# Decoder layer on one core: the order of the modulation-weight loads in the DMA queue, and a ring of 24 slots for gate tiles

## The chip, the core and the metric

The kernel runs on one core of a Trainium2 chip. The core's engines work side by side, each on its own stream of instructions: TensorE (PE in the profile; its weight loads are PEld), VectorE (DVE), ScalarE (ACT), GpSimd (POOL) and SyncE (SP). In this kernel SP only issues DMAs (the loads of weights), and POOL issues nearly all other DMAs. The metric is the device time of one launch in microseconds (us); the three runs of the kernel before took 2658.97, 2663.2 and 2664.1 us, a median of 2663.2.

## The reference

One layer of a decoder, on 512 tokens of width 2048, everything in f32:

```python
mod = silu(c) @ w_ada + b_ada            # six vectors of 2048: shift, scale, gate, twice
h = rms_norm(x, g_attn) * (1 + sc_a) + sh_a
proj = h @ w_in                          # q/k/v and indexer of A, latents of B, gate_a, gate_b
o_a = dsa_attention(...)                 # branch A: attention over selected keys
o_b = causal_dense_attention(mq, mk, mv) # branch B: 8 heads of 128 (MLA)
merged = sigmoid(gate_a) * (o_a @ w_pa) + sigmoid(gate_b) * (o_b @ w_pb)
x = x + gt_a * (merged @ w_o)
h = rms_norm(x, g_ffn) * (1 + sc_f) + sh_f
x = x + gt_f * conv_ffn(h, w_up, w_conv, b_conv, w_down)
```

`w_ada` has 2048 rows and 12,288 columns, 100 MB; `w_pb` has 1024 rows and 2048 columns.

## The kernel before

**Products.** Each f32 operand is split into a high and a low part in a form that PE multiplies at full rate, and a product is three matmuls: high by high, high by low, low by high (`mm3`, L141 to 144). Activations lie transposed in tiles of 128x512, as pairs (hi, lo); `split` (L138 copies hi on ACT, L139 subtracts for lo on DVE) makes the pair. Weights come by `wtile` (L117): SP loads a raw tile of 128x1024 at high priority (L126), ACT copies its high part (L130), DVE subtracts for the low part (L131), and the raw buffer is free again. There are five raw buffers (`rawq`) and three hi/lo pairs.

**Memory.** Everything else lies in 81 slots of 128x512 f32, handed out by `get` (L69: the free slot that has rested longest) and given back by `put`. A slot taken again makes its new writer wait for the last reader of the old contents. PSUM has eight banks.

**Stages, in the order of time in the profile.** The input projection and branch A come first; at some 633 to 767 us the gate columns are projected; then come branch B's up projections and attention, head by head, with blocks of `w_pa` between the heads (`pa_block`, whose results pa go to DRAM); from about 955 to 1107 us the second branch, that is the four blocks of `w_pb` beside the last head; then `w_o`, the second norm, the up projection with convolution, and the down projection. The last two use a scheme of seven products for eight (`seven`), with its own load of weights (`load`).

**The ada stream.** `w_ada` is multiplied by one vector only, and on DVE instead of PE: `ada_stream` (L727) is a generator that loads two tiles of 128x512 at a time and adds each, times a column of silu(c), to an accumulator (L746 the first tile, L748 the others: 0.75 us each). In the second branch and in `w_o` the tiles go to slots (L736), first through a ring of six (`ada_ring`); earlier stages use raw buffers (L740). A `ticker` advances the stream by 1.25 pairs for each weight tile of `w_pb` and `w_o`.

**The last head.** `attend_p` (L677) computes, for four query blocks (512, 384, 256, 128 keys), the scores (PE, L1225 and L1226), adds the mask and takes the row's minimum on DVE (L689), exp and row sum on ACT (L690), reciprocal (L691) and scaling (L692) on DVE. `attend_pv` (L695) transposes on PE (L700), copies out of PSUM on DVE (L703) or ACT (L705), multiplies by the values (L708, "PV" below) and splits the result (L710, L711).

**The second branch.** `load_gates(cb)` (L1268) prepares four column blocks m: it loads pa (a), the gate of A (g) and the gate of B (b) from DRAM by POOL (L1274 to 1276, ordered behind the last store of pa for cb over 0), takes the sigmoids on ACT (L1279, L1280, ordered behind the last exp) and multiplies a by g on DVE (L1281), which frees g. After the product with `w_pb`, `ev_pb` (L1286) multiplies b by the bank (L1289), adds it to a (L1290), splits the sum into the merged pair and frees both tiles. All four calls of `load_gates` together load 48 tiles.

**What sets the order.** The program is written as one sequence. A scheduler reorders it when the kernel is built: it simulates the engines' time lines and picks for each engine the next instruction by priority (a raw tile's load, copy and subtraction have a raised one) among those that could start. The order on each engine is then fixed, and on the chip each engine runs its stream strictly in order. `tc.issue_after(x)` adds an edge for that scheduler: what is traced under it stands behind x.

Of the kernel before, what the change touches and what calls it, by code (L numbers as in the profile page):

```python
# [18 lines left out]
P = 128  # L19
# [12 lines left out]
def trunk_layer_kernel(  # L32
# [21 lines left out]
    V, A, G, PE, SP = nc.vector, nc.scalar, nc.gpsimd, nc.tensor, nc.sync  # L54
# [14 lines left out]
    def get(dt=F32):  # L69

        i = min(free, key=lambda n: rested[n])
        free.remove(i)
        if cur[i] is None or cur[i].dtype != dt:
            cur[i] = pool.tile([P, T], dt, name=f"slot{i}", tag=f"slot{i}")
        held[id(cur[i])] = i
        return cur[i]
# [4 lines left out]
    def put(*ts, lag=2):  # L81

        for t in ts:
            i = held.pop(id(t))
            rested[i] = clock[0] + lag
            free.append(i)
# [23 lines left out]

    weight_bufs(5, 3, 1104)

    def r32(ap):
        return ap.bitcast(F32)


    def wtile(src, k0, kg, c0, n, pri=PRI, more=None):  # L117
        i = cnt["wt"] % len(hi_b)
        cnt["wt"] += 1
        raw = rawq.popleft()  # L120
        w = kg * n
        if more:
            w += more[1]
        hi, lo = hi_b[i][:, :w], lo_b[i][:, :w]
        with tc.high_priority(offset=pri):
            SP.dma_start(raw[:, :kg * n].rearrange("p (k n) -> p k n", k=kg),  # L126
                         src[k0 * P:(k0 + kg) * P, c0:c0 + n].rearrange("(k p) n -> p k n", p=P))
            if more:
                SP.dma_start(raw[:, n:w], src[k0 * P:(k0 + 1) * P, more[0]:more[0] + more[1]])
            A.activation(hi, raw[:, :w], AF.Copy)  # L130
            V.tensor_tensor(lo, raw[:, :w], r32(hi), ALU.subtract)  # L131
        rawq.append(raw)
        if more:
            return hi, lo
        return (hi.rearrange("p (k n) -> p k n", k=kg), lo.rearrange("p (k n) -> p k n", k=kg))
# [141 lines left out]
    for ks in (range(0, 7), range(7, 14), range(14, KD)):  # L277
# [4 lines left out]
        for k in ks:  # L282
            t = get()
# [243 lines left out]
    b = bank[7]  # L527
# [199 lines left out]
    def ada_stream():  # L727
        for n, cb in enumerate(ada_blocks):
            assert len(pend) < 3
            acc = ada_acc[n % 3]  # L730
            for kp in range(8):
                if ada_in_slots[0]:
                    ts = [ada_ring.popleft(), ada_ring.popleft()] if ada_ring else [get(), get()]
                    for i in range(2):
                        k = kp * 2 + i
                        SP.dma_start(ts[i], w_ada[k * P:(k + 1) * P, cb * 512:(cb + 1) * 512])  # L736
                else:
                    raw = rawq.popleft()
                    t = raw[:, 0:1024].rearrange("p (k n) -> p k n", k=2)
                    SP.dma_start(t, w_ada[kp * 2 * P:(kp + 1) * 2 * P, cb * 512:(cb + 1) * 512]  # L740
                                 .rearrange("(k p) n -> p k n", p=P))
                    ts = [t[:, 0], t[:, 1]]
                for i in range(2):
                    k = kp * 2 + i
                    if k == 0:
                        V.tensor_scalar(acc, ts[i], c_act[:, 0:1], None, op0=ALU.mult)  # L746
                    else:
                        V.scalar_tensor_tensor(acc, ts[i], c_act[:, k:k + 1], acc,  # L748
                                               op0=ALU.mult, op1=ALU.add)
                if ada_ring_on[0]:  # L750
                    ada_ring.extend(ts)
                elif ada_in_slots[0]:
                    put(*ts)
                else:
                    rawq.append(raw)
                yield None
            pend.append((cb, acc))
            done[0] += 1
# [44 lines left out]
    def reload(d):  # L803
# [4 lines left out]
            G.dma_start(tl, dl)  # L808
            pairs.append((th, tl))
        return pairs  # L810

    last = {}


    gate_d = [dram.tile([P, T], F32, name=f"gate{k}") for k in range(2 * KD)]
# [132 lines left out]
    def seven(work, pairs_of_banks, hook=None, AHEAD=2):  # L948
        def pair_steps(n, p):
            bx, by = pairs_of_banks[n % len(pairs_of_banks)]  # L950
            X, Y, Z = bx[:, :HT], by[:, :HT], by[:, HT:]
            L, E = {}, {}
            W = p.K * P
            g1, g2 = p.scale or (None, None)
            r11, r21, r22, t1, t2, t3, t4 = p.rs

            def done(t):
                rawq.append(t)

            def load(blk):  # L960
                t = rawq.popleft()
                SP.dma_start(t[:, :W], p.load(blk))
                return t

            def hilo(t):
                i = cnt["wt"] % len(hi_b)
                cnt["wt"] += 1
                hi, lo = hi_b[i][:, :W], lo_b[i][:, :W]
                split(hi, lo, t[:, :W])
                return hi, lo  # L970

            def comb(o, a, b, op):
                V.tensor_tensor(o[:, :W], a[:, :W], b[:, :W], op)  # L973

            def copy(o, b, g):
                if g is not None:
                    A.activation(o, b, AF.Copy, scale=g)  # L977
                else:
                    A.activation(o, b, AF.Copy)

            def plus(o, b, g):
                if g is not None:
                    V.scalar_tensor_tensor(o, b, g, o, op0=ALU.mult, op1=ALU.add)
                else:
                    V.tensor_tensor(o, b, o, ALU.add)

            def p1():
                L[11] = load(0)
                L[21] = load(1)
                return hilo(L[11])  # L990

            def p7():

                s3 = rawq.pop()
                comb(s3, L[21], L[11], ALU.subtract)
                r = hilo(s3)
                done(s3)
                L[22] = load(3)
                return r

            def p6():
                comb(L[21], L[21], L[22], ALU.add)
                comb(L[11], L[21], L[11], ALU.subtract)
                r = hilo(L[11])
                L[12] = load(2)
                return r

            def p2():
                return hilo(L[12])

            def p5():
                r = hilo(L[21])
                comb(L[12], L[12], L[11], ALU.subtract)
                done(L[11])
                done(L[21])
                return r

            def p4():
                r = hilo(L[22])
                done(L[22])  # L1020
                return r

            def p3():
                r = hilo(L[12])
                done(L[12])
                return r

            def e1():
                E["u1"] = get()
                copy(E["u1"][:, :HT], X, g1)  # L1030

            def e7():
                E["u2"] = get()
                copy(E["u2"][:, HT:], Y, g2)

            def e6():
                copy(E["u2"][:, :HT], X, g2)

            def e2():
                plus(E["u1"][:, :HT], Z, g1)  # L1040

            def e5():
                plus(E["u2"][:, HT:], X, g2)

            def e4():
                plus(E["u2"][:, :HT], Y, g2)

            def e3():
                copy(E["u1"][:, HT:], X, g1)
                p.fin(E["u1"], E["u2"])  # L1050

            return ((p1, X, r11, e1, True), (p7, Y, t3, e7, True), (p6, X, t2, e6, False), (p2, Z, r21, e2, False),
                    (p5, X, t1, e5, False), (p4, Y, t4, e4, False), (p3, X, r22, e3, False))
# [211 lines left out]
    ob = reload(ob_d) + [tuple(att["o"][0:2]), tuple(att["o"][2:4])]  # L1265
    mg = []

    def load_gates(cb):  # L1268
        ts = []
        for m in range(4):  # L1270
            j = cb * 4 + m
            a, g, b = get(), get(), get()
            with tc.issue_after(last["store"].ins) if cb else nullcontext():
                G.dma_start(a, pa_d[j])  # L1274
                G.dma_start(g, gate_d[j])
                G.dma_start(b, gate_d[KD + j])

            with tc.issue_after(last["exp"].ins):
                A.activation(g, g, AF.Sigmoid)  # L1279
                A.activation(b, b, AF.Sigmoid)  # L1280
            V.tensor_tensor(a, a, g, ALU.mult)  # L1281
            put(g)
            ts.append((a, b))
        return ts

    def ev_pb(ts):  # L1286
        def ev(m, b):
            a, g = ts[m]
            V.tensor_tensor(g, g, b, ALU.mult)  # L1289
            V.tensor_tensor(a, a, g, ALU.add)  # L1290
            hi, lo = getr(), getr()
            split(hi, lo, a)
            put(a, g)
            mg.append((hi, lo))
        return ev

# [3 lines left out]
        lin_fm(w_pb, cb * 512, ob, 8, bk, ev_pb(load_gates(cb)), tick=ticker(TB))  # L1300
    for t in ob:
        put(*t)


    ss1 = pool.tile([P, 16], F32, name="ss1x")
# [334 lines left out]
```

## Time and profile before

| what | value |
|---|---|
| three runs | 2658.97, 2663.2, 2664.1 us |
| median | 2663.2 us |
| profiled execution | 2656.78 us |
| its span, first to last instruction | 2655.0 us |
| mean granted clock of PE | 0.990 |
| PE, DVE busy | 2588.7, 2174.6 us |
| moved by DMA | 464.31 MB |

The rows below are from that one profiled execution. A group's row holds the line, engine, operation, output and inputs (slot numbers left out), and the durations in ns (least, median, most). A wait's row says which engine's instruction at which line waited for which other one, for how many us in total, how often, and at most. A time line gives start and duration in us, and in brackets the idle time of the engine just before and what ended it. x3 stands for three like instructions in a row, shown as one stretch. PEclk is the clock granted to PE, 1.00 being full speed. A DMA's landing time runs from its issue to its arrival. Matmuls are pipelined, so their durations overlap; the distance between two starts is what one costs.

### The profile page before, as it was taken

The page shows a single profiled execution, that of the slowest core. Times are in us where ns is not written, and L with a number is a line of the kernel's source. Part 1 is how long each engine was busy: PE and PEld are TensorE (multiplying, and loading weights), DVE is VectorE, ACT ScalarE, POOL GpSimd, SP SyncE. Part 2 cuts the span into 40 slices and gives each one's busy share as a digit, 9 for nine tenths or more (in the row PEclk, how much of TensorE's full clock was granted, in tenths as well). Part 3 has the DMA queues.
Part 4 walks back from the last instruction along what each step waited for, and adds up shares of the span by engine and source line. Part 5 has one row for each costly group of instructions (what it writes and reads, how often), then busy time and mean ns, then how long its engine had stood idle before and what let it go on. Part 6 is the DMA issues. An engine that isn't in the chain of part 4 may idle for free.

```text
span 2655.0 us, 44904 instructions
## 1 busy us (share of the span) xinstructions
PE 2588.7 (98%) x17168; PEld 2344.2 (88%) x17168; DVE 2174.6 (82%) x3491; ACT 1243.0 (47%) x1953; POOL 365.8 (14%) x671
## 2 busy tenths in 40 slices
PE   6999999999999999999999999999999999999999
PEld 5777687778998877888789999999999999999999
DVE  7886975779878786983669899899899889878787
ACT  4333434334445544322544555555555556655454
POOL 1000011010023223200100000000001024413120
PEclk8999899999999999999999999999999999999999
DMA  9953136774676489873324434433434447867563
GB/s 342 340 165 101 35 101 192 224 215 150 203 240 190 153 274 354 299 238 95 135 74 143 135 124 129 137 123 129 136 123 150 142 146 217 219 155 202 143 208 114
DMA packets 215661, 464.31 MB, mean 175 GB/s; under 512 B 23786, under 2 KB 65156, under 8 KB 215444
## 3 DMA queue, kind: packets, MB, share of 16 engines
q1 hardware_dynamic: 170260, 344.93, 40.4%
q0 software_dynamic: 45152, 116.50, 15.0%
q8 instruction: 134, 2.20, 0.3%
q14 instruction: 83, 0.68, 0.1%
q10 hardware_dynamic: 32, 0.01, 0.0%
HBM read 397.11 MB, written 64.23 MB: 174 GB/s over the span
## 4 chain that ended last, share of the span: by engine, by line
PE 80%; issue 7%; DMA 6%; DVE 5%; ACT 1%; POOL 1%; SPq 0%; POOLq 0%; DVEq 0%; ACTq 0%
PE bank L1077 15%; PE bank L1079 15%; PE bank L1078 15%; PE bank L142 10%; PE bank L143 10%; PE bank L144 10%; DMA slot<-in_w_ada 3%; DVE whl L139 1%; DMA x<-slot 1%; PE bank L708 1%; PE bank L903 1%; DVE slot L572 0%; DMA raw<-in_w_ada 0%; PE bank L700 0%; DMA slot<-in_x 0%
## 5 line engine op out<-in xcount | busy, mean ns | idle before, releaser
L1077 PE MATMUL bank<-slot,whl 128*128 128x256 f32 x3920 | 1102.7, 282 | 21.0 <-ACT slot L977 6.1
L1078 PE MATMUL bank<-slot,whl 128*128 128x256 f32 x3920 | 1098.9, 281 | 0.2 <-DVE slot L139 0.2
L1079 PE MATMUL bank<-slot,whl 128*128 128x256 f32 x3920 | 1088.2, 281 | 6.0 <-DVE whl L139 6.0
L138 ACT ACTIVATE whl<-raw 128x1024 fp32r<-128x1024 f32 (+2 forms) x560 | 532.6, 953 | 618.2 <-PE bank L1078 400.7
L1077 PEld LDWEIGHTS bank<-slot,whl 128*128 128x128 f32 x3920 | 738.9, 189 | 28.2 <-ACT slot L977 8.6
L1078 PEld LDWEIGHTS bank<-slot,whl 128*128 128x128 f32 x3920 | 740.1, 189 | 0.6 <-DVE slot L139 0.5
L1079 PEld LDWEIGHTS bank<-slot,whl 128*128 128x128 f32 x3920 | 732.3, 188 | 7.2 <-DVE whl L139 7.2
L139 DVE TENSOR_TENSOR whl<-raw,whl 128x1024 fp32r<-128x1024 f32 (+2 forms) x560 | 606.0, 1087 | 121.2 <-ACT whl L138 116.9
L130 ACT ACTIVATE whl<-raw 128x1024 fp32r<-128x1024 f32 (+4 forms) x182 | 187.3, 1031 | 385.6 <-PE bank L144 193.8
L973 DVE TENSOR_TENSOR raw<-raw 128x1024 f32<-128x1024 f32 (+2 forms) x320 | 347.3, 1085 | 6.7 <-DMA raw<-in_w_ups 3.7
L131 DVE TENSOR_TENSOR whl<-raw,whl 128x1024 fp32r<-128x1024 f32 (+4 forms) x182 | 215.8, 1186 | 163.7 <-ACT whl L130 162.7
L143 PE MATMUL bank<-whl,slot 128*128 128x512 f32 (+2 forms) x768 | 297.3, 388 | 0.9 <-DVE whl L131 0.9
L142 PE MATMUL bank<-whl,slot 128*128 128x512 f32 (+2 forms) x768 | 293.1, 393 | 4.3 <-ACT slot L409 3.8
L144 PE MATMUL bank<-whl,slot 128*128 128x512 f32 (+2 forms) x768 | 292.9, 385 | 0.0
L142 PE MATMUL bank<-slot,whl 128*128 128x512 f32 (+1 forms) x656 | 264.1, 407 | 6.2 <-DVE slot L703 3.8
L143 PE MATMUL bank<-slot,whl 128*128 128x512 f32 (+1 forms) x656 | 266.0, 406 | 0.1
L144 PE MATMUL bank<-slot,whl 128*128 128x512 f32 (+1 forms) x656 | 258.0, 402 | 0.0
L748 DVE SCALAR_TENSOR_TENSOR slot<-slot,c_act,slot 128x512 f32<-128x512 f32 x203 | 150.9, 747 | 46.0 <-DMA slot<-in_w_ada 44.4
L142 PEld LDWEIGHTS bank<-whl,slot 128*128 128x128 f32 x768 | 146.0, 190 | 35.6 <-ACT slot L409 3.9
L143 PEld LDWEIGHTS bank<-whl,slot 128*128 128x128 f32 x768 | 146.3, 191 | 30.0 <-DVE whl L131 1.4
L144 PEld LDWEIGHTS bank<-whl,slot 128*128 128x128 f32 x768 | 144.7, 189 | 29.4 <-issue 0.5
L142 PEld LDWEIGHTS bank<-slot,whl 128*128 128x128 f32 (+1 forms) x656 | 123.7, 189 | 37.2 <-DVE slot L703 4.2
(288 smaller groups left out, 2705.5 us busy)
## 6 DMA issues: line engine op xcount, KB each, us to landing
slot<-in_w_ada SPq DMA_DIRECT2D x344, 256.0 KB, 5.4
raw<-in_w_ups SPq DMA_DIRECT2D x160, 512.0 KB, 5.1
raw<-in_w_in SPq DMA_DIRECT2D x50, 512.0 KB, 3.7
raw<-in_w_down SPq DMA_DIRECT2D x64, 384.0 KB, 3.8
raw<-in_w_down SPq DMA_DIRECT2D x64, 320.0 KB, 3.1
slot<-f POOLq DMA_DIRECT2D x154, 128.0 KB, 4.1
f<-slot POOLq DMA_DIRECT2D x66, 256.0 KB, 5.1
raw<-in_w_gs SPq DMA_DIRECT2D x32, 512.0 KB, 3.9
```

The costliest lines, as they stand in the source:

```text
L130: A.activation(hi, raw[:, :w], AF.Copy)
L131: V.tensor_tensor(lo, raw[:, :w], r32(hi), ALU.subtract)
L138: A.activation(dst_hi, src, AF.Copy)
L139: V.tensor_tensor(dst_lo, src, r32(dst_hi), ALU.subtract)
L142: PE.matmul(o, lh, rh, start=first, stop=False)
L143: PE.matmul(o, lh, rl, start=False, stop=False)
L144: PE.matmul(o, ll, rh, start=False, stop=last)
L748: V.scalar_tensor_tensor(acc, ts[i], c_act[:, k:k + 1], acc, op0=ALU.mult, op1=ALU.add)
L973: V.tensor_tensor(o[:, :W], a[:, :W], b[:, :W], op)
L1077: PE.matmul(o, wh[:, ks], rh, start=first and k == 0, stop=False, skip_group_check=True)
L1078: PE.matmul(o, wh[:, ks], rl, start=False, stop=False, skip_group_check=True)
L1079: PE.matmul(o, wl[:, ks], rh, start=False, stop=last, skip_group_check=True)
```

## The change

Two edits. First, the SP instruction that loads the newest weight tile is kept in `last["w"]`, in `wtile` (L126) and in the load of `seven`, and each ada load into a slot (L736) is traced behind it, with an ordering edge on SP. Ada loads into raw buffers (L740) have no edge. Second, the a, g and b tiles of `load_gates` no longer come from `get()` one by one: 24 slots are taken at once into `gate_ring`, tiles are taken from its left end, and g goes back to its right end after L1281, a and b after the block's evacuation; behind the four blocks the ring is given back as a whole. All other tiles of that stage have 24 slots fewer to rotate through while the ring is held.

```diff
+    last = {}
+
...
-            SP.dma_start(raw[:, :kg * n].rearrange("p (k n) -> p k n", k=kg),
+            last["w"] = SP.dma_start(raw[:, :kg * n].rearrange("p (k n) -> p k n", k=kg),
                          src[k0 * P:(k0 + kg) * P, c0:c0 + n].rearrange("(k p) n -> p k n", p=P))
...
                     for i in range(2):
                         k = kp * 2 + i
-                        SP.dma_start(ts[i], w_ada[k * P:(k + 1) * P, cb * 512:(cb + 1) * 512])
+
+                        with tc.issue_after(last["w"].ins):
+                            SP.dma_start(ts[i], w_ada[k * P:(k + 1) * P, cb * 512:(cb + 1) * 512])
...
-    last = {}
-
...
             def load(blk):
                 t = rawq.popleft()
-                SP.dma_start(t[:, :W], p.load(blk))
+                last["w"] = SP.dma_start(t[:, :W], p.load(blk))
                 return t
...
+    gate_ring = deque(get() for _ in range(24))
+
     def load_gates(cb):
         ts = []
         for m in range(4):
             j = cb * 4 + m
-            a, g, b = get(), get(), get()
+            a, g, b = (gate_ring.popleft() for _ in range(3))
...
             V.tensor_tensor(a, a, g, ALU.mult)
-            put(g)
+            gate_ring.append(g)
             ts.append((a, b))
         return ts
...
             split(hi, lo, a)
-            put(a, g)
+            gate_ring.extend((a, g))
             mg.append((hi, lo))
         return ev
...
     for t in ob:
         put(*t)
+    put(*gate_ring)
```

## The prediction

> **What bounds the kernel now.** I read the page's line of engines first, then busy time by stage, then what TensorE (PE) waited for in the stretch that the edit touches, and at last the instructions around the longest of those waits.
>
> ```profile
> span 2655.0 us, 44904 instructions
> ...
> PE 2588.7 (98%) x17168; PEld 2344.2 (88%) x17168; DVE 2174.6 (82%) x3491; ACT 1243.0 (47%) x1953; POOL 365.8 (14%) x671
> ```
>
> PE is the bound, with 98% of the span; all the engines together can give back only the remaining 66 us. The next view holds stages: from its start in us to its end, length, busy time and instructions of each engine, granted clock, DMA share, GB/s.
>
> ```profile
> 700.00:767.00 67.00, 66.41 (x560) 66.12 (x559) 58.08 (x67) 27.62 (x36) 6.72 (x13) 1.00 0.60 192
> 860.00:955.00 95.00, 94.97 (x466) 76.79 (x465) 73.80 (x223) 47.60 (x107) 22.12 (x33) 1.00 0.54 168
> 955.00:1000.00 45.00, 44.89 (x195) 33.57 (x194) 38.45 (x75) 16.01 (x31) 8.99 (x17) 1.00 0.94 306
> 1000.00:1030.00 30.00, 28.73 (x128) 21.62 (x126) 20.39 (x44) 11.82 (x24) 15.71 (x30) 1.00 1.06 394
> 1030.00:1060.00 30.00, 26.51 (x103) 20.70 (x104) 19.42 (x29) 14.70 (x24) 6.98 (x13) 0.89 0.93 343
> 1060.00:1107.00 47.00, 47.00 (x203) 37.78 (x203) 45.76 (x70) 21.77 (x32) 14.65 (x25) 1.00 0.81 258
> 1150.00:1200.00 50.00, 50.00 (x216) 40.35 (x215) 44.73 (x65) 15.10 (x25) 0.00 (x0) 1.00 0.68 225
> 2200.00:2250.00 50.00, 45.92 (x376) 44.87 (x377) 47.72 (x76) 32.94 (x58) 17.79 (x29) 1.00 0.76 207
> ```
>
> The second branch runs from about 955 to 1107 us. PE stands still there for 1.27 us in 1000:1030 and 3.49 us in 1030:1060, and in the latter its clock falls to 0.89; just there the DMAs move 394 GB/s. Elsewhere in the table PE is full, but for 4.08 us in 2200:2250. In 1060:1107 it starts 203 matmuls in 47.00 us: 0.2315 us each, my unit for what PE can cover. PE's two waits in that stretch:
>
> ```profile
> PE bank L142 <- DVE slot L703: 3.8, 1, 3.8
> PE bank L700 <- DVE slot L692: 0.9, 1, 0.9
> ```
>
> Both belong to the last attention head. PE itself, then VectorE (DVE), then ScalarE (ACT), each row with start, duration, and in brackets the idle time before it:
>
> ```profile
> 1016.61 0.38 PE L700 MATMUL bank<-ident,slot 128*128 128x128 f32 x2
> ...
> 1028.49 0.66 PE L700 MATMUL bank<-ident,slot 128*128 128x128 f32 x4 [0.88 <-DVE slot L692]
> ...
> 1033.42 0.79 PE L142 MATMUL bank<-slot,whl 128*128 128x512 f32 x1 [3.82 <-DVE slot L703]
> 1034.01 0.63 PE L143 MATMUL bank<-slot,whl 128*128 128x512 f32 x1
> ...
> 1037.85 0.40 PE L142 MATMUL bank<-slot,whl 128*128 128x512 f32 x1
> ```
> ```profile
> 1000.09 1.22 DVE L131 TENSOR_TENSOR whl<-raw,whl 128x1024 fp32r<-128x1024 f32 x1
> ...
> 1005.58 0.74 DVE L689 CUSTOM_DVE_ANT_0 slot<-bank,slot,nsc_b 128x512 f32<-128x512 f32 x1
> ...
> 1025.63 0.75 DVE L748 SCALAR_TENSOR_TENSOR slot<-slot,c_act,slot 128x512 f32<-128x512 f32 x1 [1.52 <-DMA slot<-in_w_ada]
> 1026.30 0.15 DVE L691 RECIPROCAL ri<-su 128x1 f32<-128x1 f32 x1
> 1027.48 0.75 DVE L748 SCALAR_TENSOR_TENSOR slot<-slot,c_act,slot 128x512 f32<-128x512 f32 x1 [1.03 <-DMA slot<-in_w_ada]
> 1028.15 0.28 DVE L692 TENSOR_SCALAR slot<-slot,ri 128x128 f32<-128x128 f32 x1
> ...
> 1031.21 0.75 DVE L748 SCALAR_TENSOR_TENSOR slot<-slot,c_act,slot 128x512 f32<-128x512 f32 x1 [0.51 <-DMA slot<-in_w_ada]
> ...
> 1033.08 0.28 DVE L703 COPY slot<-bank 128x128 f32<-128x128 f32 x1
> ```
> ```profile
> 1024.45 0.19 ACT L690 ACTIVATION_READ_ACCUMULATOR slot<-slot,mn 128x1 f32 x1
> 1024.65 1.28 ACT L1280 ACT_TABLE_LOAD   x1
> ...
> 1027.53 0.62 ACT L1280 ACTIVATE slot<-slot 128x512 f32<-128x512 f32 x1
> 1028.05 0.62 ACT L1279 ACTIVATE slot<-slot 128x512 f32<-128x512 f32 x1
> ```
>
> The last exp ends at 1024.64. The reciprocal and the scaling (0.15 + 0.28 us) could follow, but two ada accumulations (L748) stand ahead of them on DVE and idle 1.52 and 1.03 us for their DMAs; so the scaling starts at 1028.15, and the copy L703 at 1033.08. PE waits for both. Why those tiles are late, from the DMA views: landing time of ada loads issued in 995:1030, of gate loads over the whole run, of gate loads in 1055:1080 when the burst is over, and the queues of 1000:1040 (packets, MB, share; q0 is POOL's, q1 SP's).
>
> ```profile
> DMA to landing us min/median/max: 7.2/12.2/17.8
> ```
> ```profile
> DMA to landing us min/median/max: 3.0/7.9/8.8
> ```
> ```profile
> DMA to landing us min/median/max: 3.0/3.0/3.1
> ```
> ```profile
> DMA packets 6340, 15.69 MB, mean 392 GB/s; under 512 B 901, under 2 KB 901, under 8 KB 6338
> ...
> q0 software_dynamic: 3323, 10.09, 66.5%
> q1 hardware_dynamic: 3015, 5.57, 38.8%
> ```
>
> An ada tile takes 12.2 us while POOL pours out pa and gate tiles; POOL gets 10.09 MB through, SP 5.57 MB.
>
> **The change, part by part.** No instruction is added or removed on any engine, and no byte; what moves is order. In the built order the streams differ on PE, DVE, ACT, POOL and SP mainly in what runs at about 633 to 1290 us, and a little at the start of the down projection.
>
> *The last head's stall.* In the changed build the last reciprocal and scaling follow the last exp with no L748 between, so the 0.88 us go. Before the copy L703 stand now two L1281 and two L748, and PE has 13 matmuls (3.0 us) between the head's last transposes and the one that needs L703's bank, against 2 before. ACT starts a sigmoid every 0.52 us after its 1.28 us table load; the second L1281 needs the seventh, which ends some 5 us after the exp. The four transposes stand 27 matmuls (6.25 us) behind the last scores, some 3 us after the exp; 3.0 us of cover more is 6 us, so L703 comes about in time. I take the 3.82 us as gone; if its two L748 wait as those above did, up to 3 us come back. With that idle stretch goes the slow clock: from 1033.42 to 1037.85 PE starts ten matmuls in 4.43 us, where ten of 0.2315 take 2.3: 2.1 us. Together −0.88 −3.82 −2.1 = **−6.8 us**.
>
> [...]
>
> *Ada loads behind the last weight load (SP).* Before, ada loads stood ahead of weight loads in SP's queue; now each waits in that queue behind the newest weight load, and that load waits for its raw buffer, freed by L131 on DVE. Queued behind it are ada tiles alone, and DVE's L748 waits for those. Between the first and the last w_pb load stand 34 ada loads, before 42; six loads that were fetched ahead of w_pb come after its first tile. These 14 tiles, 14 x 0.75 = 10.5 us of DVE work, go to the w_o stage. There, in 1150:1200, DVE is idle 5.27 of 50 us; w_o has 768 matmuls, 178 us, so about 18.8 us are free: cost nothing; without that cover at most 10.5 us.
>
> The new hazard is the last head's start: three L748 whose tiles are queued behind the eighth w_pb load now stand ahead of its first L689. That load's buffer comes free when L131 of the third w_pb tile ends, at 1001.31 by the DVE row above, and SP issues the load at once. SP's issues and the sizes:
>
> ```profile
> 1001.33 0.38 SPq L126 DMA_DIRECT2D raw<-in_w_pb  x1
> ```
> ```profile
> L736 SPq DMA_DIRECT2D slot<-in_w_ada x17: 327/328/328, 995.5 to 1028.3; - x17
> ```
> ```profile
> slot<-in_w_ada SPq DMA_DIRECT2D x16, 256.0 KB, 13.9
> ...
> raw<-in_w_pb SPq DMA_DIRECT2D x4, 512.0 KB, 13.7
> ```
>
> Add 0.4 us for its issue and 0.7 for two ada issues, the landing L, 3 x 0.75 for L748, and about 3.5 us for three L689 (0.74 the widest), exp, reciprocal and scaling: 1008.2 + L. The transposes that need it started at 1016.61 without a wait, and stand about six matmuls (1.4 us) earlier in the new order, so L over 7.0 us costs what it is over. The third tile needs 0.52 + 3 x 0.26 MB through SP: by SP's average of 5.57 MB in 40 us that is 9.4 us, by the whole 392 GB/s with a 3 us floor some 6. The ends are then 0 (L of 7.0 or less) and +10.8 (L of 17.8); I take 7.7, since at first about 16 gate and pa tiles are queued and not 36: **+0.7 us**.
>
> *The ring (POOL).* The 48 a, g and b tiles used any free slot; 24 slots hold the first 24, the rest wait for L1281, L1290 or the last head's PV to release theirs. Two chains follow the last PV. (a) The low half of the seventh w_pb tile (L131) stands on DVE now behind four L1289, two L1290 and one L1281. PE has 44 matmuls (10.2 us) and 0.4 us of small ones before it needs it. The chain starts when the second bank is full, 20 matmuls (4.6 us) after PV; seven operations at 0.68 and L131's 1.22 follow:
>
> ```profile
> L1290 DVE TENSOR_TENSOR slot<-slot,slot x14: 681/683/685, 1059.3 to 1106.3; 128x512 f32<-128x512 f32 x14
> ```
>
> That is 4.6 + 4.8 + 1.2 = 10.6, and about 0.5 for the flush and semaphores: **+0.5 us**. (b) One gate tile of the first quarter reuses a slot that this PV reads. Its landing L, then sigmoid 0.62, L1289, two L1290, L1281 and L131 make about 5.7 + L against 10.6: break-even 4.9. The row nearest is the 3.0 us of gates loaded after the burst: nothing; at the burst's 8.8 it is +3.9.
>
> *Everything else.* In the stages at 700:767, 860:955 and 1150:1200 PE is full to within 0.6 us in the rows above, whatever stands in what order on the other engines; I take 0, bounded by ±2 us. The down projection's start: 0, bounded by the 4.08 us idle of its 50 us either way.
>
> Sum: −6.8 + 0.7 + 0.5 = −5.6 us, a span of 2649.4. The profiled execution took 2656.78 us, 1.78 beyond its span, and becomes 2651.2; it lies 6.4 below the median of the three runs, so on the median **2657.6 us**.
>
> **The rivals.** *The stall stays, under another L748.* [...] Then 3 of the 3.82 us come back, with the slow clock (about 1.5 of the 2.1), and 1.2 are paid: −6.8 + 4.5 + 1.2 = −1.1, 2662.1 us. Against it: 16 instead of 36 POOL tiles in the first burst. [...]
>
> *Slower: the last head starts late.* The L748 behind the eighth w_pb load hold up L689. It decides from an ada landing of 7.0 us on, and outweighs the gain from about 13. At the 17.8 us of the worst tile before, +10.8, and the late gate tile +3.9 beside it: −6.8 + 10.8 + 3.9 + 0.5 = +8.4, 2671.6 us. For it: a median of 12.2 us in just this stretch before. Against it: those medians came with twice the POOL tiles queued.
>
> *It doesn't do what it says.* The build's order shows 34 ada loads for 42, so the edges bind; no chance of its own.
>
> **How the numbers follow.** Forecast 0.45, stall stays 0.29, late head 0.26. About 0.2% (5.3 us) is what a measurement of this kernel can tell from no change: faster is below 2657.9, slower above 2668.5. The forecast's own range, 2653 to 2661, has about 0.33 below the bound and 0.12 in it; the stall staying gives 0.04, 0.22 and 0.03; the late head, with its price from nothing to 10.8, 0.02 in the middle and 0.24 above. Rounded: faster 0.38, same 0.35, slower 0.27. The range goes from 2651 (both new terms at nothing, 2 us from other stages, and a reading 3 us low) to 2671.
>
> **What would show it.** In the changed kernel's profile: the waits L142 on L703 and L700 on L692 are gone, and the clock in 1030:1060 is 1.00; ada landing times in 995:1030 have a median below 10 us; the second branch ends near 1101 instead of 1107. Wrong: a wait of L700 on L692 or of scores on L689 early in the last head, with DVE idle before L748 (late head); a wait on L131 well over 0.5 us after the last PV (late gate); a wait on L703 of 2 us or more (the stall stays); a PE wait in w_o on what L748 holds up.

## The result, and the profile after

The changed kernel is slower: 2676.45 us (median of 6 runs, 2674.52 to 2680.13) against 2660.32 us for the kernel before in the same measurement, a ratio of 1.0064 with a 95% interval of [1.0052, 1.0076]. The forecast was 2657.6 us, a small gain, with a range from 2651 to 2671.

Lines in the changed kernel stand 3 lower up to L735, then 5 lower up to L811, then 3 again, and 6 or 7 from the gate code (L1268) on: L131 is L134, L689 to L692 are L692 to L695, L703 is L706, PV's L708 is L711, L736 is L741, L748 is L753, L793 is L798, L973 is L976, L985 is L988. First the page's two lines of the changed kernel, then its busy time by stage (columns as before).

```profile
span 2673.5 us, 44893 instructions
...
PE 2599.5 (97%) x17168; PEld 2355.0 (88%) x17168; DVE 2175.3 (81%) x3491; ACT 1243.5 (47%) x1953; POOL 367.9 (14%) x671
```
```profile
630.00:790.00 160.00, 152.89 (x1232) 149.59 (x1233) 130.81 (x151) 65.32 (x86) 13.93 (x26) 0.98 0.60 195
955.00:1000.00 45.00, 43.72 (x191) 32.71 (x189) 27.22 (x58) 14.60 (x29) 7.04 (x13) 1.00 0.83 257
1000.00:1030.00 30.00, 25.21 (x101) 18.32 (x101) 17.21 (x39) 7.35 (x16) 10.18 (x19) 0.93 0.90 297
1030.00:1060.00 30.00, 28.51 (x118) 22.45 (x119) 20.20 (x42) 18.00 (x33) 9.57 (x18) 0.90 0.74 253
```

PE runs the same 17,168 instructions, is busy 10.8 us longer (most of it is the slow clock: 0.987 granted on average against 0.990 makes about 8 us) and idle 7.7 us longer; together the 18.5 us of the span. The same stretch of the kernel before for the first row of stages:

```profile
630.00:790.00 160.00, 156.63 (x1285) 154.60 (x1285) 134.73 (x155) 67.02 (x88) 18.88 (x36) 0.98 0.66 210
```

The reader is to see two things. PE gets through 53 matmuls less in 630:790, the gate projection, a stage for which I had forecast no change. And in 1000:1030 the DMAs are less busy than before (297 GB/s, 394 before), yet PE stands still for 4.79 us where it had been 1.27. Crowded DMAs are not the trouble any more. The ada loads issued in 995:1030 land faster, too, with a median below 10 us, as the forecast had it (7.2/12.2/17.8 us before):

```profile
DMA to landing us min/median/max: 4.9/7.2/9.4
```

What counts, as the next views show, is when they are issued.

To place the loss, I compare the start of the PE instruction with the same number in both traces; both run 17,168. The table gives that difference against the kernel before in us; the column heads name the experiments below. Each column is one execution, and the first row shows scatter alone: up to 631 us the changed kernel runs the order of before.

| PE instruction (start before) | changed | e1 | e2 | e3 | e5 | e9 |
|---|---|---|---|---|---|---|
| 2500 (560) | +1.8 | -0.5 | +0.3 | +0.6 | -0.1 | +0.7 |
| 4500 (871) | +8.9 | +8.8 | +1.4 | +2.9 | -2.3 | +0.3 |
| 5000 (979) | +8.4 | +9.1 | +1.4 | +2.8 | -2.6 | +0.2 |
| 5500 (1102) | +13.2 | +9.3 | -4.4 | +5.7 | +2.9 | -7.2 |
| 13500 (2199) | +14.1 | +7.5 | -4.7 | +6.3 | +4.6 | -8.5 |
| 14000 (2265) | +18.3 | +8.7 | -2.3 | +7.8 | +5.1 | -5.9 |
| 17000 (2631) | +18.6 | +9.5 | -1.8 | +8.7 | +6.0 | -4.6 |

The changed kernel loses in three places: 7.1 us between 560 and 871 us, 4.8 between 979 and 1102 (the second branch), and 4.2 between 2199 and 2265 (the start of the down projection). `w_o`, between 1107 and 1300 us, is flat.

**The last head.** PE's waits in 955:1115 of the changed kernel:

```profile
PE bank L145 <- DVE slot L798: 4.5, 1, 4.5
PE bank L711 <- DVE slot L706: 2.7, 1, 2.7
PE bank L146 <- DVE slot L714: 0.3, 1, 0.3
```

The two waits of before (on L703's bank, and of the transposes on the scaling) are gone, as forecast; other waits have come. DVE, SP and PE around the longest, each in its own view:

```profile
1014.85 1.22 DVE L134 TENSOR_TENSOR whl<-raw,whl 128x1024 fp32r<-128x1024 f32 x1
...
1017.30 0.28 DVE L706 COPY slot<-bank 128x128 f32<-128x128 f32 x1
1024.59 0.75 DVE L753 SCALAR_TENSOR_TENSOR slot<-slot,c_act,slot 128x512 f32<-128x512 f32 x1 [7.00 <-DMA slot<-in_w_ada]
1026.52 0.75 DVE L753 SCALAR_TENSOR_TENSOR slot<-slot,c_act,slot 128x512 f32<-128x512 f32 x1 [1.18 <-DMA slot<-in_w_ada]
1028.60 0.75 DVE L753 SCALAR_TENSOR_TENSOR slot<-slot,c_act,slot 128x512 f32<-128x512 f32 x1 [1.33 <-DMA slot<-in_w_ada]
1029.27 0.74 DVE L692 CUSTOM_DVE_ANT_0 slot<-bank,slot,nsc_b 128x512 f32<-128x512 f32 x1
...
1030.47 0.69 DVE L798 TENSOR_TENSOR slot<-bank,ident 128x512 f32<-128x512 f32 x1
```
```profile
1016.10 0.38 SPq L129 DMA_DIRECT2D raw<-in_w_pb  x1
1016.52 2.82 SPq L741 DMA_DIRECT2D slot<-in_w_ada  x4
```
```profile
1031.22 0.80 PE L145 MATMUL bank<-slot,whl 128*128 128x512 f32 x1 [4.54 <-DVE slot L798]
1031.81 0.63 PE L146 MATMUL bank<-slot,whl 128*128 128x512 f32 x1
```

This is a closed loop, and it reads off the three views. DVE ends the low part of a weight tile at 1016.07; that frees the raw buffer. At 1016.10 SP, which had stood 7.0 us, issues the next weight load, and at 1016.52, behind it, the ada loads that the edge holds back. The third of the tiles that DVE needs is there only at 1028.60. DVE reaches its L748 (L753 here) at 1017.6, stands there 7.00 + 1.18 + 1.33 us, and the last head's minimum and a column flush that PE's next bank needs stand behind. Tying the load to the weight load tied it to DVE's own progress.

**The gate projection.** A like chain, near 760 us in DVE, SP and PE:

```profile
757.80 1.22 DVE L976 TENSOR_TENSOR raw<-raw 128x1024 f32<-128x1024 f32 x1
...
761.08 0.75 DVE L753 SCALAR_TENSOR_TENSOR slot<-slot,c_act,slot 128x512 f32<-128x512 f32 x1 [0.92 <-DMA slot<-in_w_ada]
764.76 0.75 DVE L753 SCALAR_TENSOR_TENSOR slot<-slot,c_act,slot 128x512 f32<-128x512 f32 x1 [2.92 <-DMA slot<-in_w_ada]
765.43 0.42 DVE L988 TENSOR_TENSOR slot<-bank,slot 128x256 f32<-128x256 f32 x1
```
```profile
759.09 0.33 SPq L965 DMA_DIRECT2D raw<-in_w_gs  x1
759.51 0.86 SPq L741 DMA_DIRECT2D slot<-in_w_ada  x2
```
```profile
765.99 0.36 PE L1080 MATMUL bank<-slot,whl 128*128 128x256 f32 x1 [2.25 <-DVE slot L988]
```

L973 (L976) ends at 759.02, the weight load follows at 759.09, the ada loads at 759.51, DVE waits for the second until 764.76, and the evacuation L985 (L988), for which PE waits, stands behind it. Here, though, the buffer is the smaller part. SP's waits in 755:764 show that SP stood 5.1 us for the store out of the slot that the ada load at 758.38 overwrites, and only 0.3 us for the buffer:

```profile
SPq L741 <- DMA gate<-slot: 5.1, 1, 5.1
SPq L965 <- DVE raw L976: 0.3, 1, 0.3
```

Such stores hold SP up in the kernel before as well (25.2 us in 630:790, 22.8 after), so this one place doesn't show what the edge costs in this stage; e1, e3 and e5 below do. What DVE idled for ada tiles in slots, in 630:790 and in 955:1107, before and then after, sums it up (us, times, longest):

```profile
DVE slot L748 <- DMA slot<-in_w_ada: 12.2, 10, 4.7
...
DVE slot L748 <- DMA slot<-in_w_ada: 13.6, 10, 3.4
```
```profile
DVE slot L753 <- DMA slot<-in_w_ada: 19.7, 15, 2.9
...
DVE slot L753 <- DMA slot<-in_w_ada: 27.1, 10, 7.0
```

### The profile page after: what moved, and what is told of

The parts are those of the page before. It is cut to its first block, busy times and chain, and to the rows that moved or that the text cites. A ratio compares the mean times of both kernels' runs of the same rounds, so it can differ in the third digit from the quotient of the medians.

```text
span 2673.5 us, 44893 instructions
## 1 busy us (share of the span) xinstructions
PE 2599.5 (97%) x17168; PEld 2355.0 (88%) x17168; DVE 2175.3 (81%) x3491; ACT 1243.5 (47%) x1953; POOL 367.9 (14%) x671
## 4 chain that ended last, share of the span: by engine, by line
PE 64%; DVE 5%; DMA 5%; issue 2%; ACT 1%; POOL 0%; SPq 0%; DVEq 0%; ACTq 0%; POOLq 0%
PE bank L1080 15%; PE bank L1081 15%; PE bank L1082 15%; PE bank L145 6%; PE bank L146 6%; PE bank L147 6%; DMA slot<-in_w_ada 3%; DVE whl L142 2%; DVE raw L976 1%; DMA x<-slot 1%; ACT whl L141 1%; PE bank L1229 1%; PE bank L1228 1%; DVE slot L753 0%; PE bank L711 0%
## 5 line engine op out<-in xcount | busy, mean ns | idle before, releaser
L976 DVE TENSOR_TENSOR raw<-raw 128x1024 f32<-128x1024 f32 (+2 forms) x320 | 348.0, 1088 | 7.2 <-DMA raw<-in_w_ups 4.2
L133 ACT ACTIVATE whl<-raw 128x1024 fp32r<-128x1024 f32 (+4 forms) x182 | 187.1, 1030 | 350.8 <-PE bank L147 188.1
L134 DVE TENSOR_TENSOR whl<-raw,whl 128x1024 fp32r<-128x1024 f32 (+4 forms) x182 | 216.7, 1191 | 139.3 <-ACT whl L133 138.2
L753 DVE SCALAR_TENSOR_TENSOR slot<-slot,c_act,slot 128x512 f32<-128x512 f32 x203 | 151.7, 750 | 82.4 <-DMA slot<-in_w_ada 80.8
```

Source lines behind the costliest of these rows:

```text
L753: V.scalar_tensor_tensor(acc, ts[i], c_act[:, k:k + 1], acc, op0=ALU.mult, op1=ALU.add)
```

## The experiments

**Which part, and where.** Four kernels. In e1 the edge holds only until the second branch and there is no ring; e2 is the ring alone; e3 is the changed kernel with the edge only from the second branch on; e4 has both places of the edge and no ring.

```diff
 e1, e3 (condition on the edge; e1 has "not", e1 and e4 also take the ring out)
-                        with tc.issue_after(last["w"].ins):
+                        with tc.issue_after(last["w"].ins) if not ada_ring_on[0] else nullcontext():
```

> Only the ada loads of the gate projection (633 to 767 us) stand behind the last weight load; the second branch, w_o and the gate tiles are as before. Theory (three separate losses, one of them there): about 2660.3 + 6.5 = 2667 us, all of it gained between the matmuls that stood at 617 and 775 us before, and the difference constant after that. Rival (the ring and what follows from it make the whole loss, and that stage's loss in the one profile was chance): 2660, within 0.2%.

Measured: 2665.37 us, ratio 1.0031 [1.0019, 1.0044]; the table has the whole loss before 871 us. DVE's idle time for ada tiles in 630:790 and in 955:1107:

```profile
DVE slot L753 <- DMA slot<-in_w_ada: 21.3, 13, 5.4
...
DVE slot L753 <- DMA slot<-in_w_ada: 13.3, 9, 3.2
```

The first is close to that of the changed kernel (19.7), the second to that of before (13.6). The edge alone makes that stage's loss, without the ring.

How much one execution says can be read off the kernels that run this stage in one and the same order. With the edge, the start of instruction 4500 against that of 2500 moves by +7.1 us (changed), +9.3 (e1), +8.7 (e4), +12.8 (e6) and +12.1 (e10); without it, against the kernel before, by +1.1 (e2) and +2.3 (e3). The loss is clear of the scatter; its size is known to some 3 us only.

> Only the ring of 24 slots; no ada load is ordered behind a weight load. Theory (the ordering edges make the losses before 1107 us): the gate projection is as before, the last head keeps about the 6.8 us of before, and at the start of the down projection the order differs, for 0 to +4 us: 2658 to 2665. Rival (the ring's late tiles and the 24 slots taken from the rest make the loss): 2668 or more, with PE waits after the last PV.

Measured: 2653.91 us, ratio 0.9987 [0.9977, 0.9997]: the ring is a gain, where the theory had expected the last head to keep its 6.8 us. The rival falls. In the second branch 5.8 us are won (+1.4 to -4.4). The same two idle times (L748 is L751 here), then the queues in 1000:1040:

```profile
DVE slot L751 <- DMA slot<-in_w_ada: 12.1, 11, 4.4
...
DVE slot L751 <- DMA slot<-in_w_ada: 4.5, 4, 2.9
```
```profile
q1 hardware_dynamic: 4222, 7.82, 55.6%
q0 software_dynamic: 2398, 7.22, 47.6%
```

POOL's tiles come in portions: 7.22 MB instead of 10.09, and SP gets 7.82 through instead of 5.57. So in this trace SP moves more where POOL moves less; in that of e11 below it does not, with 7.19 MB for POOL and 5.21 MB for SP.

> The changed kernel without the ordering edge in the gate projection; edge in the second branch and w_o, and the ring, as changed. Theory: 2676.5 - 6.5 = 2670 us, with the waits of the last head at about 1018 to 1031 us as in the changed kernel (4.5 us and the slow clock after it). Rival (that stage is not the cause): 2676.

Measured: 2662.64 us, ratio 1.0020 [1.0011, 1.0029], 7 us better than my number. The last head's 4.5 us wait is there in full. What I had not reckoned with is that the changed kernel's 4 us at the start of the down projection are here only 1.5.

> Both ordering edges' places, no ring. The order on DVE at the last head is that of the changed kernel: three L748 ahead of the first L689. Theory: gate projection +6.5, last head +4.5, start of the down projection 0 to +4: 2671 to 2675 us. With 36 and not 16 gate and pa tiles queued in the burst, the three L748 could wait longer than the changed kernel's 7.0 + 1.2 + 1.3 us: then above 2675. Rival (ring): 2662.

Measured: 2670.6 us, ratio 1.0052 [1.0040, 1.0065], a hair under the theory. By ratios: the edge in the gate projection costs 0.31%, the two edges without the ring 0.52%, so the second branch's edge some 0.2%, while the ring without the edge wins 0.13%. The parts don't simply add: beside the ring the second branch's edge costs 0.33% (e3 against e2), and the changed kernel, which has ring and edges, is no faster than e4.

**Is it the distance of the edge?** e5 keeps the edge in all places and the ring, but points it one weight load further back.

```diff
-            last["w"] = SP.dma_start(...)
+            last["w0"], last["w"] = last.get("w"), SP.dma_start(...)
...
-                        with tc.issue_after(last["w"].ins):
+                        with tc.issue_after(last["w0"].ins):
```

> The changed kernel, but each ada load stands behind the weight load before the last one, one weight tile looser. Theory (the edge makes ada loads wait for a raw buffer, so they are issued late, and DVE, in order, stands idle at L748 with the work behind it that PE needs): issues come one weight tile earlier, some 4 us in the gate projection and 8 us at the last head; there the waits on L985 go, with 4 of its 8 us, and the last head's 4.5 us wait shrinks below 2: 2665 to 2669 us. Rival (the mere shuffling of the orders costs, wherever the edge points): 2674 or more.

Measured: 2660.86 us, ratio 1.0010 [1.0001, 1.0018], better than the theory's number. The two idle times:

```profile
DVE slot L753 <- DMA slot<-in_w_ada: 12.9, 13, 2.1
...
DVE slot L753 <- DMA slot<-in_w_ada: 27.6, 11, 4.6
```

In the gate projection the idle time is back at the 12 us of before, and the stage's loss with it (-2.3 at the 4500th instruction). One weight tile of distance is the whole difference there; the rival, that any edge's shuffling costs, falls for this stage. In the second branch my expectation failed: DVE still idles 27.6 us, and waits of 3.8 and 1.9 us on L703 (L706) stand in PE's list:

```profile
PE bank L145 <- DVE slot L706: 3.8, 1, 3.8
PE bank L1228 <- DVE slot L706: 1.9, 1, 1.9
```

**Is it the place of the three L748?** e6 moves them on DVE only, behind the last head's third scaling.

```diff
+            m = V.tensor_scalar(p, p, ri, None, op0=ALU.mult)
+            if qb == 1:
+                last["scale"] = m
...
+    nring, NR = [0], 15
...
+                        if ada_ring_on[0]:
+                            nring[0] += 1
+                        with tc.issue_after(last["scale"].ins) if nring[0] > NR else nullcontext():
+                            V.scalar_tensor_tensor(acc, ts[i], c_act[:, k:k + 1], acc,
```

> The changed kernel with one more ordering edge, on DVE alone: from the 16th L748 of the second branch on, L748 stands behind the last head's third scaling (L692), so the three L748 with late tiles move behind its L689, the column flush L793 and three L692. Theory: PE's 4.5 us wait on L793 and the 2.1 us of slow clock after it go, a wait of 0 to 2 us at what now stands behind the L748 (L711, L131, L703) comes: 2676 - 5 = 2671 us. Rival (the last head is late for its weights or its gate tiles): 2676, the wait at the same place.

Measured: 2675.49 us, ratio 1.0060 [1.0046, 1.0073]: nothing won. PE's waits in 940:1130:

```profile
PE bank L145 <- DVE slot L708: 3.5, 1, 3.5
PE bank L713 <- DVE slot L708: 2.7, 1, 2.7
PE bank L1234 <- DVE slot L716: 2.2, 1, 2.2
PE bank L146 <- DVE slot L716: 2.1, 1, 2.1
```

The wait on the column flush is gone, as the theory has it, but 2.2 and 2.1 us on the split L711 (L716 here) and 3.5 on the copy L703 (L708) have come, where I had allowed 2 us in all. In this trace the late tiles cost wherever DVE meets them; the place only decides who waits. (The profiled execution took 2682.05 us, 6.6 above the median, so the single waits may be long ones.)

**Without DVE's wait.** In e7 and e8 the L748 up to the end of the gate projection read their own accumulator instead of the loaded tile, e7 with e1's edge, e8 without; the sums of those columns are left out.

```diff
+                        src = acc if ada_in_slots[0] and not ada_ring_on[0] else ts[i]
-                        V.scalar_tensor_tensor(acc, ts[i], c_act[:, k:k + 1], acc,
+                        V.scalar_tensor_tensor(acc, src, c_act[:, k:k + 1], acc,
```

> The kernel of the first experiment (edge in the gate projection alone), and there the L748 read their own accumulator and not the loaded tile: same DVE time, same loads, but no L748 waits for a DMA; the sums of those columns are left out. Theory (DVE stands idle for late ada tiles): the 7.7 us over the kernel before go, 2657 us or less, within 2 us of the next run. Rival (the edge makes the weights of that stage late, or the shuffled order costs by itself): 2662 to 2666, PE waiting at the same places.

> The kernel before with the same replacement in L748 up to the end of the gate projection (own accumulator instead of the loaded tile; those sums are left out), as the base of the run above. Before, DVE idled 11.3 us at L748 in 640 to 800 us without a PE wait on it but for 2.7 us at 775. Theory: 2655 to 2658 us, little change. Rival: 2650 or less, if PE had been waiting behind L748 in more places than the waits name.

Measured: e7 2668.07 us, ratio 1.0037 [1.0025, 1.0049]; e8 2676.65 us, ratio 1.0065 [1.0052, 1.0079]. Neither theory's number holds, and the pair says nothing on the edge: a tile that nobody reads leaves its slot to the next load at once, all five engines run another order than the kernel before, and in e8's SP waits of 630:790 ada loads wait 29.5 us for earlier ada loads (3.9 in the kernel before):

```profile
SPq L736 <- DMA slot<-in_w_ada: 29.5, 16, 3.3
```

**The two gains together.** e9 has the ring, the looser edge of e5 up to the second branch, and no edge from there on.

```diff
-                        with tc.issue_after(last["w"].ins):
+                        with tc.issue_after(last["w0"].ins) if not ada_ring_on[0] else nullcontext():
```

> The ring of 24 slots, and in the gate projection alone ada loads behind the weight load before the last one; in the second branch and w_o no edge. Theory (losses add by stage): the ring's -3.8 us and the -2 to -2.6 us that the looser edge showed up to 980 us make 2651 to 2653 us, faster than both kernels; DVE idles about 13 us at L748 in 630 to 790, and the last head's waits stay near 1 us. Rival (each build's order is a draw of its own, stages don't add): anywhere from 2653 to 2662.

Measured: 2650.92 us, ratio 0.9969 [0.9959, 0.9979], faster than both kernels and, against its number, just where the theory put it. PE's only wait in 940:1130 (L713 is L710):

```profile
PE bank L145 <- ACT slot L713: 0.4, 1, 0.4
```

The split of the gain is not what I had said, though: by the table it is all the second branch's, 7.4 us, and nothing shows at the 4500th instruction. e2 and e9 differ by 0.18% with intervals that just touch; whether the looser edge gains on its own stays open. What the pair of e9 and e5 does show is the second branch's edge: the two differ in nothing else, and with it the ratio is 1.0010 instead of 0.9969. So there the edge costs even when it is one weight tile looser; why the distance mends the gate projection and not this stage stays open.

**The start of the down projection.** In the changed kernel DVE stands there for a store from a slot that is to be overwritten, with the evacuation L983 (L986) behind it, for which PE waits 2.07 us until 2265.10; half-speed matmuls follow (clock 0.57 in 2265:2269):

```profile
2258.75 0.83 DVE L976 TENSOR_TENSOR raw<-raw 128x640 f32<-128x640 f32 x1
2262.49 1.42 DVE L142 TENSOR_TENSOR slot<-slot,slot 128x512 fp32r<-128x512 f32 x2 [2.92 <-DMA x<-slot]
...
2264.57 0.48 DVE L986 SCALAR_TENSOR_TENSOR slot<-bank,mod,slot 128x256 f32<-128x256 f32 x1
```

e10 gives such slots a longer rest.

```diff
-            put(*us, lag=6)
+            put(*us, lag=10)
```

> The changed kernel with one size altered: a result tile of the down projection rests 10 steps instead of 6 before its slot is taken again (lag of put). Theory (the 4.2 us lost at 2235 to 2265 us are a slot taken while the store of its old tile is still on the way: DVE stood 2.92 us for it at L139 with L983 behind): DVE's wait on that store goes, and 2 to 4 of the 4.2 us: 2673 us. Rival (chance of the one profile, or the order of PE there): the same 4 us lost, 2676; with the other order of slots it may also come back elsewhere in the down projection.

Measured: 2674.6 us, ratio 1.0067 [1.0053, 1.0081]. The wait on the store is gone from DVE's list, but PE now waits 5.2 us in 2180:2330 for high parts on ACT (3.0 in the changed kernel), in an execution of 2682.76 us, 8.2 above the median, and nothing is won:

```profile
PE bank L1080 <- ACT whl L141: 5.2, 4, 2.2
```

So the wait is shown, but not that it is the price: which slots are met there is a by-product of what was taken and given back before, and each build draws another hand (+0.5 to +4.2 us between the 13500th and the 14000th instruction in the table).

**A smaller ring.** e11 is e2 with 16 slots.

> The ring alone with 16 slots instead of 24. Theory (the ring gains because fewer POOL tiles are queued at once while SP's ada tiles are awaited): 16 slots queue 12 tiles or so at first, ada tiles land in 995:1030 in 7.4 us or less, DVE idles 4.5 us or less for them in 955:1107, and the gates of the later quarters come later without holding up PE: 2652 to 2655 us. Rival (the gain is the order's, not the queue's): 2657 or more; or gate tiles become late, with a PE wait after the last PV on what L1281 and L1290 hold up.

Measured: 2653.22 us, ratio 0.9981 [0.9972, 0.9990]: the time was as expected, the reason only in part. The ada loads issued in 995:1030 landed, in e2 and then in e11:

```profile
DMA to landing us min/median/max: 5.9/7.4/11.3
```
```profile
DMA to landing us min/median/max: 7.0/10.3/11.2
```

10.3 us are close to the 12.2 of before, and in 1000:1040 SP gets 5.21 MB through, no more than the 5.57 of before. DVE's idle time for ada tiles in slots fell all the same: at L748 (L751 here) 6.8 us, 4.5 in e2 and 13.6 before, and with the first tile of each block (L746, L749 here) 7.5, 8.2 and 15.2 us. So neither the landing time nor what SP gets through sets the time alone. Both rings share that POOL moves 7.2 MB in 1000:1040, but in the slow changed kernel it moves only 5.23. Whether the ring gains by thinner traffic or by the order that came with it was not taken apart.

## Why the prediction was wrong, step by step

Two steps failed. "Everything else" was put at 0 and cost 7.1 us in the gate projection and 4.2 at the start of the down projection; and the second branch, put at -5.6 us in all, came to +4.8, because the late head was mis-sized and what goes with it was left out. The late head was named as a rival, but even its worst price, +8.4, is half of the 16 us measured.

- **The last head's stall goes, -6.8 us.** Right in the mechanism: with L691 and L692 right behind the exp, both waits are gone. But the edge was not what the gain needed: the ring alone gets it (e2).
- **The late head, +0.7 us.** The mechanism was right, and it was a rival with its point of decision; its size was wrong. My landing time was 7.7 us. Measured from the end of L131 to the third L748, 1016.07 to 1028.60, it is 12.5 us; less the 1.1 for issuing, the tile is there 11.4 us on. My own formula, landing less 7.0, then gives 4.4, and PE waited 4.54. That they meet so closely is luck: the low part that I had at 1001.31 ended 14.8 us later, and PE waited at the column flush that stands behind the same three tiles, and not at the transposes. I took an average of SP's share and discounted it for a shorter POOL queue, when the nearest row was the median of 12.2.
- **What went with it was left out.** The head before it suffers the same: PV waits 2.71 us on L703 behind other late tiles. And both waits bring the slow clock (0.90 in 1030:1060, where I had named 1.00 as a sign). Ten matmuls at half speed follow the long one (2.1 us), and some five follow the 2.71 us one. Waits of 2.7 + 4.5 + 0.3 and the slow clock of 2.1 and about 1.4 make 11.0 us, against 6.8 before: +4.2, and the trace has +4.8.
- **"Everything else", 0 within ±2 us.** This step failed. I argued from PE's full rows in 700:767 that no order on the other engines mattered there. But the edge holds in that stage too, and PE is full only as long as DVE keeps up; in 630:790 DVE idled 12.2 us for ada tiles before, of which one stretch of 4.69 us made PE wait 2.70 us (until 779.00), and 19.7 us after, where PE's waits on DVE are 6.3 us against 3.3. e1 measures the step: +0.31%, about 8 us.
- **Ada loads in w_o, 0.** Right: the table is flat through `w_o`, with 14 more tiles in it.
- **The low part after the last PV, +0.5, and the late gate tile, 0.** Right within what can be read: no wait on L131 there, and 0.3 us on L711. The 5.7 us of the late gate tile are too many, though: the six operations named add up to 4.6 by the rows.
- **The start of the down projection, 0 within 4.08 us.** Outside by a little: 4.2 us, in the changed kernel alone among the columns; the 2.07 us wait and a half-speed stretch behind it of 3.4 us, some 1.7 us of loss, make up most of it.
- **The clock.** Of the waits in 1000:1060 of the kernel before, the one of 3.82 us was followed by the slow clock (0.50 granted in 1034:1037) and the one of 0.88 us was not (1.00 in 1028.90:1029.40); the late head's price had no slow clock in it. But shorter waits than 3.82 us bring it as well. In the changed kernel half speed followed a wait of 2.71 us (below) and also waits of 2.25 and 2.07 us (until 765.99 and 2265.10), and in the kernel before, where I had overlooked them, waits of 2.70 and 2.33 us (until 779.00 and 1298.87). A wait of 2.73 us in the changed kernel (until 617.91) was followed by full speed, and so was one of 2.11 us in the kernel before (until 615.49). So in these traces waits of two microseconds could cost more than themselves, and their length alone did not decide it.

```profile
1001.43 0.49 PE L711 MATMUL bank<-slot,slot 128*128 128x128 f32 x2 [2.71 <-DVE slot L706]
...
1003.57 0.63 PE L146 MATMUL bank<-slot,whl 128*128 128x512 f32 x1
```

## What to carry to other kernels

An ordering edge between two loads hands the second one everything that the first waits for; if that is a buffer which a compute engine frees, and the same engine then waits for the second load, the flight of the DMA can lie open in each round (here SP stood 7.0 us for the buffer, and DVE then 7.00 + 1.18 + 1.33 us for the tiles). Check an edge in every stage where it holds, by the idle time of the engine that consumes the load (in 630:790 it went from 12.2 to 19.7 us), and not by whether the bounding engine looks full. What gained here was the ring without the edge in the second branch (0.9987, with 16 slots 0.9981, with the looser edge in the gate projection 0.9969), by a way that stays open. And a wait in one profile is one execution's: the same order lost 7 to 13 us in the gate projection.

## What the hardware showed

The DMAs were less loaded in the slower kernel (297 against 394 GB/s in 1000:1030), and the tiles still came later for their consumer, since they were asked for later (DVE idled up to 7.0 us for one in 955:1107, before 3.4). And whether a wait of some 2 to 3 us brings the slow clock differs from execution to execution: all thirteen traces have one and the same wait of 2.32 to 2.33 us at about 1300 us, and six to nine matmuls at half speed follow it in ten of them, none in e1, e4 and e9 (clock 0.83 in 1299:1309 of the kernel before, 1.00 in 1291:1301 of e9).
